# Subtractions and weighted sums on VectorE: one operation over 1024 columns in place of two over 512

## The chip, the cores and the metric

The kernel runs on one core of a Trainium2 chip. The time is device microseconds (us) of one execution; for the kernel before it is 1416.0 us, the median of 3 runs (1414.63 to 1416.56). A change is measured against runs of the kernel before on the same chip.

## The reference

Two layers of one mixer each, on 256 latent tokens and 256 context tokens of 2048 features, all float32:

```python
shift, scale, gate = jnp.split(sc @ w_ada[l] + b_ada[l], 3, axis=-1)       # the same for c_ctx
h_lat = rms_norm(x, norm_g[l]) * (1.0 + scale[:, None]) + shift[:, None]
h_ctx = rms_norm(xc, norm_g[l]) * (1.0 + scale_c) + shift_c
p = h @ w_in                                   # q, k, v, g_gqa, cq, ckv, kr, g_mla
...
o_a = block_attention(q, concat(ctx k, lat k), concat(ctx v, lat v))         # GQA, 8 heads
o_b = block_attention(q_mla, ...)                                            # MLA, 8 heads
x = x + gate[:, None] * (concat(o_a * silu(g_a), o_b * silu(g_b)) @ w_out)
```

In layer 0 the context tokens pass through the same mixer, in layer 1 only their keys and values are needed. A final `rms_norm` ends it. The vectors `shift`, `scale` and `gate` (the modulation) depend on two vectors alone, `c` and `c_ctx`, multiplied by a matrix of 2048 x 6144 per layer.

## The kernel before

**Matmuls in three parts.** Each float32 operand is split into a high part, rounded to the matmul's float32r, and a low part, the rest. `mm3` (L138) issues three matmuls for one product: high by high (L141), and the two mixed ones (L142, L143). A weight tile is made by `wtile` (L105): one DMA of 512 KB into a `raw` buffer (4 buffers), `hi` by a copy on ScalarE (L114, 3 buffers), and `lo = raw - hi` (L116, 2 buffers). The tile has k * w columns per partition, mostly 2 x 512 = 1024, in 48 tiles 2 x 288 = 576, and 512 in the first tiles. `lo` is computed in two halves, two instructions of the same line, each over half the columns. Every fifth tile's `lo` is computed on GpSimd (POOL), the others on VectorE (DVE).

**The modulation in the background.** The first part of layer 0's modulation runs on TensorE at the start (`ada_pe`, L229). Everything else of it, layer 0's gate and all of layer 1's modulation, is a matrix by vector product on DVE (`ada_half`, L252): a row block of the transposed matrix is loaded into a `rad` buffer (128 x 1024, 512 KB, 2 buffers), and for each vector v (two of them, one for layer 1's gate) the products with `cb[:, v]` are summed along the row. This is line L273, one instruction with an accumulator, in NG = 2 halves of 512 columns: the first writes its sum to `o`, the second takes `o` as its start value. Each instruction is followed by a short one that reads the accumulator out. 128 `rad` blocks make 224 sums, so 448 instructions and 448 reads. The products themselves go to a `junk` tile that nobody reads.

**What sets the order.** `ada_rest` is a generator. `wtile` advances it by `bg_rate` steps per weight tile (1.3 in most of layer 0, 0.4 in layer 1), which fixes the place of the sums in the order in which the program is written. A scheduler then orders all instructions by a simulation of its own (`schedule_with_timeline_sim`): on each engine, and on the one DMA queue (SP), an instruction is put where the simulation finds it ready. At run time each engine and the queue take their instructions strictly in that order. A `rad` or `raw` load waits on SP for the last reader of the buffer that it fills, and what is behind it on SP waits too.

**Other names.** `pt` (L147, L148) is the transposed softmax split in two, `p` (L600, L603) the softmax, whose scaling by 1/sum runs on POOL, `sm` (L597, L598, L601) its maxima and sums on DVE, `go` (L810) the gated output projection, `rb` and `ra` (L469, L471) rotary products, `y_d` a store of the finished GQA output, `gate_d` the gates in DRAM. The layer 0 stages in order: input projections by slices of the features (0 to about 230 us), GQA heads beside the remaining projections (230 to 480), MLA projections and heads, and the output projection (to about 835), then layer 1.

Of the kernel before, what the change touches and what calls it, by code (L numbers as in the profile page):

```python
# [35 lines left out]
NB_ACC, NB_ATT = 4, 4  # L36
FILL = (1, 0, 1, 0, 1, 1, 1, 0)
POOL_LO = 5
NG = 2

BGS, BG0, BG1, BG3, BG2 = 5.0, 1.3, 1.1, 0.5, 0.4
TCKW = {"schedule_with_timeline_sim": True}
# [2 lines left out]
def fr(ap):  # L45
    return ap.bitcast(F32)


class Net:
# [55 lines left out]
    def wtile(self, src, k, w):  # L105
        nc = self.nc
        self.nw += 1
        t = self.raw(src, k, w, "rad" if self.start and self.nw % 3 == 0 else "raw")[0][:, : k * w]
        h = self.wp.tile([P, 1024], F32R, tag="hi", name=self.nm("hi"))[:, : k * w]
        lo = self.wp.tile([P, 1024], F32R, tag="lo", name=self.nm("lo"), bufs=NB_LO)[:, : k * w]  # L110
        self.nlo += 1
        e = nc.gpsimd if POOL_LO and self.nlo % POOL_LO == 0 else nc.vector
        n = k * w
        nc.scalar.copy(h, t)  # L114
        for c in (slice(0, n // 2), slice(n // 2, n)):
            e.tensor_tensor(out=lo[:, c], in0=t[:, c], in1=fr(h[:, c]), op=ALU.subtract)  # L116
        self.bg_due += self.bg_rate
        while self.bg and self.bg_due >= 1.0:
            self.bg_due -= 1.0
            self.bg_step()  # L120
        if not self.bg:
            self.bg_due = 0.0
        v = lambda z: z.rearrange("p (k n) -> p k n", k=k)
        return v(h), v(lo)
# [127 lines left out]
    def ada_half(self, half, work):  # L252
# [8 lines left out]
        for l, kind, vs in work:  # L261
# [4 lines left out]
            for k in range(KT):  # L266
                r = self.raw(self.a["w_adaT"][r0 + k * P : r0 + (k + 1) * P, hs], 1, 1024, "rad")[1][:, 0, :]
                for v in vs:
                    o = out[:, k, v : v + 1]
                    for i in range(NG):  # L270
                        cs = slice(i * 1024 // NG, (i + 1) * 1024 // NG)
                        junk = self.tp.tile([P, 1024 // NG], BF16, tag="junk", name=self.nm("junk"), bufs=1)
                        nc.vector.tensor_tensor_reduce(  # L273
# [924 lines left out]
```

## Time and profile before

| | |
|---|---|
| median of 3 runs | 1416.0 us |
| profiled execution, whole | 1413.77 us |
| its span, first to last instruction | 1412.0 us |
| mean granted TensorE clock | 0.984 |
| PE busy | 1331.6 us, 94% |
| DVE busy | 1094.0 us, 77% |
| ACT busy | 602.6 us, 43% |
| POOL busy | 404.0 us, 29% |
| DMA | 272.47 MB, mean 193 GB/s |

Busy times are unions of the instructions' spans on one engine. Matmuls overlap, so a busy PE is not always one at its full pace; the idle time of PE and a granted clock under 1 are what it certainly lost. [...]

### The profile page before, as it was taken

What the parts mean: (1) busy time and instruction counts of PE and PEld (TensorE: products, weight loads), DVE (VectorE), ACT (ScalarE), POOL (GpSimd) and SP (SyncE); (2) the same over time, 40 slices, a digit from 0 to 9 for tenths busy, and PEclk for the clock granted to TensorE, in tenths of its full rate; (3) what the DMA queues carried; (4) which work ended last, traced back from release to release, by engine and by line L of the source; (5) the groups of instructions that cost most, each with busy time, mean ns of one, the idle gap of its engine ahead of it and who ended that gap; (6) DMA issues with size and microseconds to landing.
All of it is one profiled execution on the core that took longest, in us unless ns stands there. A gap on an engine that the chain in (4) does not pass through costs nothing.

```text
span 1412.0 us, 21026 instructions
## 1 busy us (share of the span) xinstructions
PE 1331.6 (94%) x7516; PEld 1128.1 (80%) x7516; DVE 1094.0 (77%) x2297; ACT 602.6 (43%) x974; POOL 404.0 (29%) x385
## 2 busy tenths in 40 slices
PE   5999999999997999898998999999999999999996
PEld 4776787877786987787886778898898989888884
DVE  2776548998887998989998965976787776857566
ACT  4322224535443242455532134665555644454443
POOL 0110015423223130221222213533234431223335
PEclk9999999999999999999999999999999999999999
DMA  9987733455554766443576665655775757733444
GB/s 310 354 276 268 271 104 104 135 164 181 160 187 155 209 217 199 148 147 120 179 247 210 209 214 178 202 161 169 237 257 162 237 156 259 257 108 124 157 139 144
DMA packets 142120, 272.47 MB, mean 193 GB/s; under 512 B 8336, under 2 KB 53824, under 8 KB 140608
## 3 DMA queue, kind: packets, MB, share of 16 engines
q1 hardware_dynamic: 142016, 271.13, 59.5%
q8 instruction: 59, 0.97, 0.3%
q14 instruction: 45, 0.37, 0.1%
HBM read 264.78 MB, written 6.32 MB: 192 GB/s over the span
## 4 chain that ended last, share of the span: by engine, by line
PE 55%; DVE 21%; DMA 11%; issue 6%; ACT 3%; POOL 2%; SPq 1%; DVEq 0%; POOLq 0%; ACTq 0%
PE acc L143 16%; PE acc L141 16%; PE acc L142 15%; DVE junk L273 8%; DMA rad<-in_w_adaT 7%; DVE lo L116 5%; PE att L592 3%; PE att L229 2%; PE att L615 1%; DMA raw<-in_w_in 1%; DMA cb<-in_cr 1%; DVE sm L597 1%; DVE pt L148 1%; DMA ra<-in_w_ada 1%; ACT hi L114 1%
## 5 line engine op out<-in xcount | busy, mean ns | idle before, releaser
L114 ACT CAST hi<-raw 128x1024 fp32r<-128x1024 f32 (+2 forms) x279 | 271.9, 977 | 380.1 <-PE acc L142 206.4
L116 DVE TENSOR_TENSOR lo<-raw,hi 128x512 fp32r<-128x512 f32 (+2 forms) x446 | 307.5, 731 | 88.8 <-PE acc L143 39.5
L116 POOL TENSOR_TENSOR lo<-raw,hi 128x512 fp32r<-128x512 f32 (+2 forms) x112 | 153.4, 1390 | 466.1 <-PE acc L143 317.4
L141 PE MATMUL acc<-hi,h 128*128 128x512 f32 (+1 forms) x672 | 239.3, 359 | 7.4 <-ACT cq L455 4.8
L142 PE MATMUL acc<-hi,h 128*128 128x512 f32 (+1 forms) x672 | 237.7, 356 | 0.0
L273 DVE CUSTOM_DVE_ANT_0 junk<-rad,cb 128x512 bf16<-128x512 f32 x224 | 175.0, 781 | 76.0 <-DMA rad<-in_w_adaT 50.4
L143 PE MATMUL acc<-lo,h 128*128 128x512 f32 (+1 forms) x672 | 227.4, 359 | 2.7 <-DVE lo L116 2.4
L273 DVE CUSTOM_DVE_ANT_0 junk<-rad,cb,as 128x512 bf16<-128x512 f32 x224 | 193.1, 862 | 3.8
L142 PE MATMUL acc<-h,lo 128*128 128x512 f32 (+1 forms) x512 | 171.4, 340 | 2.5 <-DVE lo L116 2.5
L143 PE MATMUL acc<-h,hi 128*128 128x512 f32 (+1 forms) x512 | 170.0, 338 | 0.0
L603 POOL TENSOR_SCALAR p<-p,sm 128x512 f32<-128x512 f32 (+1 forms) x96 | 85.8, 900 | 283.9 <-DVE sm L601 247.9
L141 PE MATMUL acc<-h,hi 128*128 128x512 f32 (+1 forms) x512 | 165.0, 341 | 0.3 <-ACT q L455 0.3
L143 PE MATMUL acc<-lo,y 128*128 128x512 f32 x384 | 146.3, 400 | 9.2 <-DVE lo L116 8.1
L141 PE MATMUL acc<-hi,y 128*128 128x512 f32 x384 | 150.7, 398 | 2.4 <-ACT y L147 2.0
L142 PE MATMUL acc<-hi,y 128*128 128x512 f32 x384 | 151.9, 396 | 0.2 <-DVE y L148 0.2
L141 PEld LDWEIGHTS acc<-hi,h 128*128 128x128 f32 x672 | 127.2, 189 | 28.9 <-ACT cq L455 5.0
L143 PEld LDWEIGHTS acc<-lo,h 128*128 128x128 f32 x672 | 124.6, 189 | 22.3 <-DVE lo L116 4.1
L142 PEld LDWEIGHTS acc<-hi,h 128*128 128x128 f32 x672 | 127.0, 189 | 15.5
L142 PEld LDWEIGHTS acc<-h,lo 128*128 128x128 f32 x512 | 96.8, 190 | 12.8 <-DVE lo L116 3.6
L143 PEld LDWEIGHTS acc<-h,hi 128*128 128x128 f32 x512 | 96.7, 190 | 9.8
L141 PEld LDWEIGHTS acc<-h,hi 128*128 128x128 f32 x512 | 93.6, 190 | 13.0 <-issue 2.5
L143 PEld LDWEIGHTS acc<-lo,y 128*128 128x128 f32 x384 | 73.4, 192 | 28.0 <-DVE lo L116 12.2
(219 smaller groups left out, 2281.4 us busy)
## 6 DMA issues: line engine op xcount, KB each, us to landing
rad<-in_w_adaT SPq DMA_DIRECT2D x128, 512.0 KB, 4.5
raw<-in_w_in SPq DMA_DIRECT2D x125, 512.0 KB, 4.5
raw<-in_w_out SPq DMA_DIRECT2D x72, 512.0 KB, 4.0
ra<-in_w_ada SPq DMA_DIRECT2D x32, 1024.0 KB, 8.4
raw<-in_w_in SPq DMA_DIRECT2D x48, 288.0 KB, 3.1
raw<-in_w_ukv SPq DMA_DIRECT2D x16, 512.0 KB, 3.5
cb<-in_cr SPq DMA_DIRECT2D x6, 1024.0 KB, 7.2
raw<-in_w_uq SPq DMA_DIRECT2D x12, 512.0 KB, 3.7
```

The costliest lines, as they stand in the source:

```text
L114: nc.scalar.copy(h, t)
L116: e.tensor_tensor(out=lo[:, c], in0=t[:, c], in1=fr(h[:, c]), op=ALU.subtract)
L141: mm(out, lhsT=ah, rhs=bh, start=first, stop=False)
L142: mm(out, lhsT=al, rhs=bh, start=False, stop=False)
L143: return mm(out, lhsT=ah, rhs=bl, start=False, stop=last)
L148: self.nc.vector.tensor_tensor(out=lo, in0=src, in1=fr(hi), op=ALU.subtract)
L229: nc.tensor.matmul(ps[32 * g : 32 * g + 32, :], lhsT=self.scp[:, m + i, o : o + 32], rhs=rs[kind, m][:, i, :], start=run is runs[0] and j ...
L273: nc.vector.tensor_tensor_reduce(out=junk, in0=r[:, cs], in1=cb[:, v, cs], scale=1.0, scalar=o if i else 0.0, op0=ALU.mult, op1=ALU.add, a ...
L592: self.order = nc.tensor.matmul(banks[j], lhsT=q[:, qs], rhs=k[:, ks], start=i == 0, stop=i == len(score) - 1)
L597: nc.vector.tensor_reduce(out=nb[:, c], in_=v, axis=AX.X, op=ALU.max)
L603: nc.gpsimd.tensor_scalar(out=pr[j], in0=pr[j], scalar1=l[:, j : j + 1], scalar2=1.0, op0=ALU.mult, op1=ALU.mult)
L615: nc.tensor.transpose(b[:, k, j * P : (j + 1) * P], pr[j][:, (i + k) * P : (i + k + 1) * P], self.ident)
```

## The change

Three edits. On DVE `lo` is computed by one instruction over all k * w columns; on POOL it stays in two halves. NG is 1, so that a sum takes one instruction over 1024 columns and one accumulator read, the start value is always 0.0, and `junk` is 1024 columns wide (2 KB per partition, before 1 KB). The scratch memory for DMA descriptors is set to 2 KB per partition; no DMA of this kernel is issued by POOL.

```diff
-NG = 2
+NG = 1
...
         e = nc.gpsimd if POOL_LO and self.nlo % POOL_LO == 0 else nc.vector
         n = k * w
         nc.scalar.copy(h, t)
-        for c in (slice(0, n // 2), slice(n // 2, n)):
+        for c in (slice(0, n // 2), slice(n // 2, n)) if e is nc.gpsimd else (slice(0, n),):
             e.tensor_tensor(out=lo[:, c], in0=t[:, c], in1=fr(h[:, c]), op=ALU.subtract)
...
-    nc = bacc.Bacc("TRN2", target_bir_lowering=False, num_devices=1)
+    nc = bacc.Bacc("TRN2", target_bir_lowering=False, num_devices=1, dynamic_dma_scratch_size=2048)
```

Since the scheduler simulates the program, the order changes on every engine. The first place is the DMA queue SP in the middle of the GQA heads of layer 0, around the store of the first GQA group (`y_d_94`); `cb` are the vectors of the next group of sums. Before:

```order
L827 DMA lg_3680<-in_lat_gain 128x512
L96 DMA raw_3542<-in_w_in 128x2x512
L96 DMA rad_2702<-in_w_adaT 128x1024
L942 DMA y_d_94<-g_63_382 128x2048
L96 DMA rad_2743<-in_w_adaT 128x1024
L96 DMA rad_2784<-in_w_adaT 128x1024
L96 DMA raw_3583<-in_w_in 128x2x512
L96 DMA rad_2828<-in_w_adaT 128x1024
L96 DMA raw_3624<-in_w_in 128x2x512
L259 DMA cb_2825<-in_cr 128x2x1024
```

And the same place on SP now:

```order
L96 DMA raw_3358<-in_w_in 128x2x512
L96 DMA rad_2691<-in_w_adaT 128x1024
L96 DMA rad_2730<-in_w_adaT 128x1024
L96 DMA raw_3394<-in_w_in 128x2x512
L827 DMA lg_3514<-in_lat_gain 128x512
L259 DMA cb_2727<-in_cr 128x2x1024
L96 DMA rad_2736<-in_w_adaT 128x1024
L942 DMA y_d_94<-g_63_379 128x2048
L96 DMA rad_2772<-in_w_adaT 128x1024
L96 DMA rad_2808<-in_w_adaT 128x1024
L96 DMA raw_3431<-in_w_in 128x2x512
```

The second `cb` load stood behind the store and now stands in front of it: the background has moved ahead of the projections. Counted over the whole queue, 14 `rad` loads from the matrix stood ahead of this store and now 18, 29 and now 38 ahead of the second group's store, and 74 and now 90 ahead of the reload of `y_d` shortly before the output projection, at 41, 51 (now 53) and 94 `raw` loads.

The second place is DVE in the output projection of layer 0, from the last `go` of its first 512 columns to the next `lo`. Before:

```order
L810 TENSOR_TENSOR go_7303<-acc_6822,gt_6790 128x512
L273 ISA junk_6394,as_4354<-rad_6392,cb_5007 128x512
L273 ISA as_4354 128x1
L273 ISA junk_6396,as_4354<-rad_6392,cb_5007,as_4354 128x512
L273 ISA as_4354 128x1
L273 ISA junk_6398,as_4354<-rad_6392,cb_5007 128x512
L273 ISA as_4354 128x1
L273 ISA junk_6400,as_4354<-rad_6392,cb_5007,as_4354 128x512
L273 ISA as_4354 128x1
L273 ISA junk_6404,as_4354<-rad_6402,cb_5007 128x512
L273 ISA as_4354 128x1
L116 TENSOR_TENSOR lo_7392<-raw_7389,hi_7391 128x512 x2
```

And the same place on DVE now, from the second `go` on:

```order
L810 TENSOR_TENSOR go_6827<-acc_6376,gt_6361 128x512
L810 TENSOR_TENSOR go_6838<-acc_6383,gt_6359 128x512
L810 TENSOR_TENSOR go_6850<-acc_6390,gt_6359 128x512
L273 ISA junk_7035,as_4109<-rad_7033,cb_4688 128x1024
L273 ISA as_4109 128x1
L273 ISA junk_7037,as_4109<-rad_7033,cb_4688 128x1024
L273 ISA as_4109 128x1
L116 TENSOR_TENSOR lo_6933<-raw_6930,hi_6932 128x1024
```

Five halves from two `rad` blocks stood between the last `go` and `lo`; now it is two whole sums from one block. Between the four `go`s of this step stood six halves of sums and one pair for `lo`; now there is one `lo` and no sum.

## Rows read from the trace of the kernel before

**Rows 1.** The page, part 1: busy us (share of span) and instructions.
```profile
PE 1331.6 (94%) x7516; PEld 1128.1 (80%) x7516; DVE 1094.0 (77%) x2297; ACT 602.6 (43%) x974; POOL 404.0 (29%) x385
```

**Rows 2.** Windows: stretch; us; PE, PEld, DVE, ACT, POOL busy (x); PE clock; DMA share; GB/s.
```profile
230.00:480.00 250.00, 232.46 (x1228) 198.18 (x1227) 222.23 (x528) 107.55 (x172) 83.34 (x80) 0.97 0.53 167
480.00:835.00 355.00, 332.98 (x1753) 281.81 (x1752) 318.99 (x752) 135.60 (x236) 81.10 (x77) 0.98 0.59 190
835.00:1230.00 395.00, 385.39 (x2371) 344.62 (x2370) 294.63 (x544) 203.63 (x309) 142.56 (x133) 1.00 0.65 208
```

**Rows 3.** Waits of PE, 480 to 835: total us, times, longest us.
```profile
PE acc L143 <- DVE lo L116: 6.9, 4, 3.2
PE acc L141 <- DVE rb L471: 4.7, 2, 2.5
PE att L592 <- ACT p L600: 2.9, 1, 2.9
```

**Rows 4.** Waits in 230 to 480, of PE and of DVE.
```profile
PE att L615 <- POOL p L603: 5.4, 6, 1.8
...
DVE junk L273 <- ACT cb L260: 13.2, 2, 7.9
```

**Rows 5.** The page, part 5: groups xcount | busy us, mean ns | idle before, releaser.
```profile
L116 DVE TENSOR_TENSOR lo<-raw,hi 128x512 fp32r<-128x512 f32 (+2 forms) x446 | 307.5, 731 | 88.8 <-PE acc L143 39.5
...
L273 DVE CUSTOM_DVE_ANT_0 junk<-rad,cb 128x512 bf16<-128x512 f32 x224 | 175.0, 781 | 76.0 <-DMA rad<-in_w_adaT 50.4
```

**Rows 6.** Timeline of DVE, 565 to 573: start us, us, instruction.
```profile
565.29 1.29 DVE L116 TENSOR_TENSOR lo<-raw,hi 128x512 fp32r<-128x512 f32 x2
...
567.17 0.69 DVE L469 TENSOR_TENSOR ra<-acc,k 128x512 f32<-128x512 f32 x1
567.77 0.75 DVE L471 TENSOR_TENSOR rb<-acc,k 128x256 f32<-128x256 f32 x2
568.43 0.68 DVE L273 CUSTOM_DVE_ANT_0 junk<-rad,cb 128x512 bf16<-128x512 f32 x1
...
569.04 3.47 DVE L116 TENSOR_TENSOR lo<-raw,hi 128x512 fp32r<-128x512 f32 x2
```

**Rows 7.** Timeline of POOL, 565 to 573.
```profile
568.59 3.36 POOL L663 TENSOR_TENSOR tw<-ra,rb 128x512 f32<-128x512 f32 x2 [19.04 <-DVE rb L471]
```

**Rows 8.** Timeline of DVE, 766 to 774.
```profile
766.06 0.69 DVE L273 CUSTOM_DVE_ANT_0 junk<-rad,cb 128x512 bf16<-128x512 f32 x1
...
766.80 0.75 DVE L273 CUSTOM_DVE_ANT_0 junk<-rad,cb,as 128x512 bf16<-128x512 f32 x1
767.47 0.08 DVE L273 DVE_READ_ACCUMULATOR2_ANT as<- 128x1 f32 x1
...
769.21 2.34 DVE L116 TENSOR_TENSOR lo<-raw,hi 128x512 fp32r<-128x512 f32 x2
```

**Rows 9.** Windows for line L273 alone: DVE busy us (x, accumulator reads included).
```profile
230.00:480.00 250.00, 128.60 (x311) 0.97 0.53 167
480.00:835.00 355.00, 184.36 (x463) 0.98 0.59 190
```

**Rows 10.** Timeline of PE, 770 to 775.
```profile
771.00 0.50 PE L143 MATMUL acc<-lo,y 128*128 128x512 f32 x1 [3.23 <-DVE lo L116]
...
773.24 0.63 PE L141 MATMUL acc<-hi,y 128*128 128x512 f32 x1
773.67 0.63 PE L142 MATMUL acc<-hi,y 128*128 128x512 f32 x1
```

**Rows 11.** Waits of PE, 835 to 1412.
```profile
PE acc L143 <- DVE lo L116: 2.6, 4, 0.9
PE acc L142 <- DVE lo L116: 2.5, 4, 0.9
```

**Rows 12.** All waits for a rad load, and rad's times from issue to landing.
```profile
DVE junk L273 <- DMA rad<-in_w_adaT: 50.4, 39, 4.2
...
DMA to landing us min/median/max: 3.4/4.6/11.4
```

## The prediction, made before the result was known

> **What bounds the kernel now.** I read the page's first part, then the windows by stage, then the waits of PE in each stage, and last the instructions around the longest waits. The first part shows two engines close to full: PE is busy for 1331.6 of 1412.0 us, DVE for 1094.0 [rows 1]. A shorter DVE instruction is worth something only where PE waits for DVE, so the windows decide. From 835 to 1230 us PE is idle for 395 - 385.4 = 9.6 us at full clock, with DVE at three quarters: nothing to gain there. From 230 to 480 DVE is busy for 222.2 of 250 us, from 480 to 835 for 319.0 of 355, and PE loses there 17.5 and 22.0 us idle, besides the clock: a mean grant of 0.97 and 0.98 costs up to 0.03 x 250 = 7.5 and 0.02 x 355 = 7.1 us [rows 2]. So about 54 us lie on the table in these 605 us, and only the part that DVE causes can go.
>
> What DVE causes is seen in the waits. From 480 to 835 PE waits 6.9 us for `lo`, 4.7 for `rb`, and 2.9 for a softmax that had waited for its inputs [rows 3]; from 230 to 480 the largest wait is 5.4 us for `p`, scaled on POOL as soon as DVE has its sum [rows 4]. One such wait is worth more than its length: at 771.00 PE resumes after 3.23 us without work, and shortly after it issues a matmul every 0.43 us (773.24 to 773.67), with a duration of 0.63 in place of 0.50 or less [rows 10]. That is the lower of the clock's two levels, given after the gap and kept for a while.
>
> **The change part by part.** First the price of one operation. A 512 column operation holds DVE for 567.77 - 567.17 = 0.60 us, two of 256 columns for 568.43 - 567.77 = 0.66 us, so 0.33 each [rows 6]. The 256 further columns cost 0.27 us and the start of an instruction 0.06. An operation of 1024 columns then takes 0.60 + 0.54 = 1.14 us, two halves 1.20. There are 446 / 2 = 223 pairs of `lo` on DVE [rows 5], so this part saves 223 x 0.06 = 13 us of DVE's time over the whole kernel.
>
> [...]
>
> The sums gain more per pair. Two adjacent halves take 766.80 - 766.06 = 0.74 us for the first, since the second waits for its start value, and 767.47 - 766.80 = 0.67 for the second, together 1.41 [rows 8]. A half with another operation behind it takes 569.04 - 568.43 = 0.61 [rows 6]; halves that stand apart cost 0.61 + 0.67 = 1.28. No operation of 1024 columns with an accumulator is in this trace; from the rows it takes 0.61 + 0.54 = 1.15. The saving is 0.13 to 0.26 per sum, with bounds of 0 (if the accumulating operation were slower over long rows) and 0.8 (the mean of 0.781 for one half [rows 5] vanishing whole). I take 0.19, the middle, because both patterns are frequent: 224 x 0.19 = 43 us. Together DVE is freed of about 56 us of 1094.
>
> What happens beside POOL is not saved. With POOL idle a pair of `lo` takes 1.29 us, beside POOL's `tw` 3.47 [rows 6, 7]. Each half seems to wait once for one POOL instruction, 2.18 / 2 = 1.1 us. As long as DVE has work, each POOL instruction will meet one DVE instruction, long or short, so I count the same total of such waits and no gain; POOL will wait 0.54 us longer per meeting.
>
> Now where the time falls. By the order on SP the sums move ahead: 38 blocks instead of 29 are queued ahead of the second group's store, 90 instead of 74 ahead of the output projection. So in the GQA heads, up to that store, 9 more blocks, or 18 more sums, of 1.15 us are to be done, +21 us. The 311 / 4 = 78 sums already there [rows 9] save 78 x 0.13 to 0.26 = 10 to 20. On balance DVE gets 1 to 11 us more work in the stretch where it is already at 222 of 250. Some of it fits into DVE's own idle time (13.2 us of waiting for `cb` alone [rows 4]). I charge 5 us to PE here.
>
> From 480 to 835 both effects add: 116 sums before [rows 9], about 18 of them gone and the rest shorter by 0.19, so DVE loses 18 x 1.34 + 98 x 0.19 = 43 us of 319. Then most of PE's waits for DVE go. In the output projection five halves stood between the last `go` and the `lo` for which PE waited at 767.8; now two whole sums do, 2.3 us in place of 0.61 x 5 = 3.1 plus the wait for one more block, and the four `go`s have none between them, where six halves stood. I let the 6.9 us of `lo` go, half of `rb`'s 4.7 (its rest is POOL's), none of the 2.9, which hangs on a load of `cb`, 2 us of the small ones behind DVE, and 5 of the 7.1 us of clock that these gaps caused: 6.9 + 2.4 + 2 + 5 = 16 us.
>
> Against it stands the first half of `lo`. At 769.21 the pair of `lo` starts and lasts to 771.55, PE resumes at 771.00, so it waits for the first half alone [rows 8, 10]. With one operation its columns are free 0.54 us later. Where PE waits for `lo` with nothing to spare, 8 times after 835 [rows 11], that adds up to 8 x 0.54 = 4.3 us; I take 2, and 1 back for the shorter sums in front. The start and the end of the kernel have no sums and few waits for DVE: 0. Sum: -16 + 5 + 1 = -10 us, from the profiled 1413.8 to 1403.8. The median of the runs shown is 2.2 us above that execution, so 1406 us.
>
> **The rivals.** A: the freed time turns into waiting for `rad`. DVE waits 50.4 us in 39 places for such loads, and one takes 4.6 us to land [rows 12]. With two buffers a block can come every (4.6 + two sums) / 2: (4.6 + 2.7) / 2 = 3.65 us before, (4.6 + 2.3) / 2 = 3.45 after. Where this loop sets the pace, only 0.2 of the 0.4 us saved per block remains; and as DVE is in order, each wait holds back the `lo` and `pt` behind it. The blocks come thicker than before, which speaks for it; from 230 to 835 DVE was held by its own work more than by loads, which speaks against. Half of the 16 us gone, with the 6 us of charges unchanged: 1413 to 1418.
>
> B: slower, through the GQA heads. Here the change puts up to 11 us more work on DVE, the blocks come one every 3 to 4 us, and softmax, `pt` and `lo` stand behind whole sums. If DVE is the bound there and loads add 9 blocks x 1.1 us of waiting, PE loses 11 + 10 = 21 us, less some 9 us that it had lost already; with gaps of 3 us the lower clock adds 3, which makes +15. With 11 of the 16 us from 480 to 835 kept and the 1 us of the late halves, the sum is +5, and with 6 kept it is +10: 1421 to 1426. It decides from the point where PE's idle time from 230 to the last store grows by more than the gain behind it. For it speaks DVE's 89% there, against it that PE's waits in this stretch are on several engines.
>
> C: POOL pays. POOL's scaling of `p` and every fifth `lo` would be late by 0.54 us per meeting. With the 6 waits for `p` [rows 4] and as many elsewhere it costs 12 x 0.54 = 6.5 us, leaving -3.5: 1412.5 us. [...]
>
> **How the numbers follow.** A change under 0.2% (2.8 us) is not told from none, so faster means under 1413.2 and slower over 1418.8. The forecast, with 1398 to 1411, has 0.5; C 0.08, most of it faster; a larger gain, all 29 us of idle and clock from 480 to 835, down to 1387, 0.05; A 0.17, with nearly all of it no change; B 0.2. That gives faster 0.60, same 0.19, slower 0.21. The range for 8 in 10 reaches from 1391 to 1422: it leaves out the far end of the large gain and of B.
>
> **What would show it.** In the profile after, L116 on DVE at about 1.2 us (with POOL active 2.2) and L273 at about 1.2; DVE busy near 1040; from 480 to 835 PE's waits for `lo` under 2 us and a granted clock of 0.99 or more; the stretch up to the second store as long as before or 5 us longer. I am wrong if PE's idle time grows in the GQA heads by more than 10 us, if DVE's waits for `rad` rise over 80 us, or if L273's mean is over 1.6 us, which means that length cost more than the columns.

## The result: slower by 0.7%

The changed kernel takes 1427.59 us (median of 4 runs, 1425.72 to 1428.33), the kernel before beside it 1415.32 (1413.98 to 1416.56). The ratio is 1.007, 95% interval 1.0046 to 1.0094, so 12 us lost where 10 were forecast as gained, and outside the range. The profiled execution has a span of 1426.2 us.

The page's first part after the change, against [rows 1]:

```profile
PE 1333.6 (94%) x7516; PEld 1130.8 (79%) x7516; DVE 991.1 (69%) x1618; ACT 602.5 (42%) x974; POOL 434.7 (30%) x385
```

DVE has 1094.0 - 991.1 = 102.9 us less to do, almost twice the 56 us of the forecast, and POOL 30.7 more. PE does the same work, and the kernel is longer. The windows by stage, against [rows 2]:

```profile
230.00:480.00 250.00, 227.75 (x1147) 190.45 (x1146) 218.23 (x375) 103.55 (x167) 98.76 (x83) 0.95 0.56 177
480.00:835.00 355.00, 330.80 (x1799) 285.28 (x1799) 269.34 (x459) 135.56 (x238) 85.42 (x76) 0.98 0.56 180
```

In the first row PE got through 1147 matmuls in place of 1228, and the granted clock fell from 0.97 to 0.95. In the traces of both kernels the grant at any moment is 1.00 or 0.50, and a value between them is a mean of the two: before, behind the gap of [rows 10], it is 1.00 up to 772 us, 0.50 from 773 to 775, and 1.00 again from 776. Windows by the clock on the wall compare different work once the kernels have drifted apart, so I cut the kernel at two instructions that both have: the second store to `y_d` (end of the GQA heads) and the first matmul of L386 (layer 1's norm). The rows are those of one source line each, with its first and last start; of L942 I take the last, of L386 the first. Before:

```profile
L942 SPq DMA_DIRECT2D y_d<-g x2: 330/376/423, 326.3 to 413.5; - x2
...
L386 PE MATMUL att<-k,xn x64: 270/272/275, 888.0 to 926.2; 128*128 128x128 f32 x64
```

After:

```profile
L942 SPq DMA_DIRECT2D y_d<-g x2: 330/334/338, 336.1 to 441.3; - x2
...
L386 PE MATMUL att<-k,xn x64: 270/273/328, 901.2 to 937.6; 128*128 128x128 f32 x64
```

Up to the second store the kernel lost 441.3 - 413.5 = 27.8 us. From there to layer 1's norm it gained: 901.2 - 441.3 = 459.9 in place of 474.5, so 14.6. From there to the end 525.0 in place of 524.0.

The two cuts don't hold quite the same work, as the windows of PE show (matmuls in the first bracket). Before:

```profile
0.00:413.50 413.50, 385.04 (x2150) 304.91 (x2151) 311.46 (x672) 159.60 (x258) 99.53 (x106) 0.98 0.64 208
413.50:888.00 474.50, 444.93 (x2319) 378.41 (x2319) 402.96 (x924) 175.77 (x295) 117.79 (x108) 0.97 0.59 190
```

After, and two matmuls from a stretch at the full clock (445 to 455 us, granted clock 1.00):

```profile
0.00:441.30 441.30, 402.34 (x2183) 317.32 (x2184) 320.39 (x562) 162.61 (x260) 108.99 (x106) 0.96 0.65 211
441.30:901.20 459.90, 431.56 (x2286) 370.07 (x2285) 331.33 (x534) 170.60 (x290) 126.06 (x107) 0.98 0.56 181
```

```profile
449.02 0.39 PE L142 MATMUL acc<-hi,h 128*128 128x512 f32 x1
449.25 0.39 PE L143 MATMUL acc<-lo,h 128*128 128x512 f32 x1
```

In the changed kernel 33 matmuls of the projections have moved in front of the second store. At one every 0.23 us that is, as an estimate, 7.6 us of work, so on equal work some 20 us are lost in front of the store and some 7 gained behind it. In front of it PE's idle time grew from 28.5 to 39.0 us, and the clock's fall from 0.98 to 0.96 costs up to 0.04 x 441.3 - 0.02 x 413.5 = 9.4 us more, an estimate as well.

What stood there, by PE's waits from 230 to 480, against [rows 4]:

```profile
PE att L615 <- POOL p L603: 6.9, 6, 2.3
PE att L143 <- DVE pt L148: 5.0, 3, 3.0
PE att L592 <- DVE qT L148: 4.9, 1, 4.9
```

Of these the wait for `qT` is new. The one for `pt` was smaller before:

```profile
PE att L143 <- DVE pt L148: 2.2, 2, 1.1
```

One timeline of DVE shows how the wait for `pt` comes about (start us, us, instruction):

```profile
314.83 2.07 DVE L273 CUSTOM_DVE_ANT_0 junk<-rad,cb 128x1024 bf16<-128x1024 f32 x1
...
316.97 2.17 DVE L273 CUSTOM_DVE_ANT_0 junk<-rad,cb 128x1024 bf16<-128x1024 f32 x1
...
319.18 1.60 DVE L273 CUSTOM_DVE_ANT_0 junk<-rad,cb 128x1024 bf16<-128x1024 f32 x1
...
320.92 1.49 DVE L273 CUSTOM_DVE_ANT_0 junk<-rad,cb 128x1024 bf16<-128x1024 f32 x1
...
322.35 0.41 DVE L623 TENSOR_TENSOR g<-att,g 128x256 f32<-128x256 f32 x1
...
323.28 1.21 DVE L273 CUSTOM_DVE_ANT_0 junk<-rad,cb 128x1024 bf16<-128x1024 f32 x1
...
324.50 1.21 DVE L116 TENSOR_TENSOR lo<-raw,hi 128x1024 fp32r<-128x1024 f32 x1
325.63 0.68 DVE L148 TENSOR_TENSOR pt<-att,pt 128x512 fp32r<-128x512 f32 x1
326.23 1.21 DVE L273 CUSTOM_DVE_ANT_0 junk<-rad,cb 128x1024 bf16<-128x1024 f32 x1
327.37 0.08 DVE L273 DVE_READ_ACCUMULATOR2_ANT as<- 128x1 f32 x1
```

Four sums stand in front of the gating `g`, a fifth and a `lo` in front of `pt`, with no idle time between. PE waits for both, 0.41 us for `g` and 2.98 for `pt`; the last row is its later wait for `qT`:

```profile
322.90 0.36 PE L141 MATMUL att<-pt,v 128*128 128x256 f32 x1 [0.41 <-DVE g L623]
...
326.36 0.39 PE L143 MATMUL att<-pt,v 128*128 128x256 f32 x1 [2.98 <-DVE pt L148]
...
342.98 1.65 PE L592 MATMUL att<-kT,qT 128*128 128x512 f32 x3 [4.90 <-DVE qT L148]
```

The wait for `qT` goes back to the `cb` load that has moved in front of the store, as the order on SP had shown. DVE and ScalarE, one after the other:

```profile
335.66 0.42 DVE L623 TENSOR_TENSOR g<-att,g 128x256 f32<-128x256 f32 x1 [0.40 <-PE att L143]
341.09 1.23 DVE L273 CUSTOM_DVE_ANT_0 junk<-rad,cb 128x1024 bf16<-128x1024 f32 x1 [5.00 <-ACT cb L260]
...
342.24 1.28 DVE L148 TENSOR_TENSOR qT<-att,qT 128x512 fp32r<-128x512 f32 x2
```

```profile
337.85 1.28 ACT L260 ACT_TABLE_LOAD   x1 [3.31 <-DMA cb<-in_cr]
339.14 1.91 ACT L260 ACTIVATE cb<-cb 128x2048 f32<-128x2048 f32 x1
340.96 1.54 ACT L147 CAST qT<-att 128x512 fp32r<-128x512 f32 x3
```

ScalarE stands for the load, the casts of `qT` behind it; DVE stands at a sum that needs `cb`, with the `qT` for which PE waits queued behind that sum.

### The profile page after: what moved, and what is told of

The parts are those of the page before. It is cut to its first block, busy times and chain, and to the rows that moved or that the text cites. A ratio compares the mean times of both kernels' runs of the same rounds, so it can differ in the third digit from the quotient of the medians.

```text
span 1426.2 us, 20239 instructions
## 1 busy us (share of the span) xinstructions
PE 1333.6 (94%) x7516; PEld 1130.8 (79%) x7516; DVE 991.1 (69%) x1618; ACT 602.5 (42%) x974; POOL 434.7 (30%) x385
## 4 chain that ended last, share of the span: by engine, by line
PE 56%; DVE 17%; DMA 10%; issue 6%; POOL 5%; ACT 3%; SPq 1%; DVEq 0%; POOLq 0%; ACTq 0%
PE acc L141 16%; PE acc L142 16%; PE acc L143 16%; DVE junk L273 7%; DMA rad<-in_w_adaT 5%; DVE lo L116 3%; PE att L592 3%; DMA cb<-in_cr 2%; PE att L229 2%; POOL lo L116 1%; PE att L615 1%; DMA raw<-in_w_in 1%; DVE sm L597 1%; DVE pt L148 1%; DMA ra<-in_w_ada 1%
## 5 line engine op out<-in xcount | busy, mean ns | idle before, releaser
L273 DVE CUSTOM_DVE_ANT_0 junk<-rad,cb 128x1024 bf16<-128x1024 f32 x224 | 297.3, 1327 | 99.0 <-DMA rad<-in_w_adaT 71.2
L116 DVE TENSOR_TENSOR lo<-raw,hi 128x1024 fp32r<-128x1024 f32 (+2 forms) x223 | 266.2, 1196 | 138.6 <-PE acc L143 69.5
L116 POOL TENSOR_TENSOR lo<-raw,hi 128x512 fp32r<-128x512 f32 (+2 forms) x112 | 147.3, 1336 | 419.3 <-PE acc L143 256.1
L143 PE MATMUL acc<-lo,h 128*128 128x512 f32 (+1 forms) x672 | 224.1, 359 | 5.3 <-DVE lo L116 4.1
L603 POOL TENSOR_SCALAR p<-p,sm 128x512 f32<-128x512 f32 (+1 forms) x96 | 102.6, 1075 | 293.3 <-DVE sm L601 239.7
L141 PEld LDWEIGHTS acc<-hi,y 128*128 128x128 f32 x384 | 72.1, 188 | 19.4 <-ACT y L147 2.8
```

Of the source, the lines that this page charges most:

```text
L141: mm(out, lhsT=ah, rhs=bh, start=first, stop=False)
L143: return mm(out, lhsT=ah, rhs=bl, start=False, stop=last)
L273: nc.vector.tensor_tensor_reduce(out=junk, in0=r[:, cs], in1=cb[:, v, cs], scale=1.0, scalar=o if i else 0.0, op0=ALU.mult, op1=ALU.add, a ...
L603: nc.gpsimd.tensor_scalar(out=pr[j], in0=pr[j], scalar1=l[:, j : j + 1], scalar2=1.0, op0=ALU.mult, op1=ALU.mult)
```

## The experiments

Ratios are against runs of the kernel before on the same chip. "Order" is the sequence of the instructions on each engine, as the scheduler drew it or as the kernel fixes it.

| | operations | order | us | ratio, 95% |
|---|---|---|---|---|
| after | whole | drawn | 1427.6 | 1.007 (1.0046 to 1.0094) |
| e1 | `lo` whole | drawn | 1421.1 | 1.0031 (1.0019 to 1.0043) |
| e2 | sums whole | drawn | 1423.0 | 1.0039 (1.0014 to 1.0063) |
| e3 | whole | drawn, other rates | 1436.9 | 1.0158 (1.0129 to 1.0188) |
| e4 | halves | drawn (as before) | 1415.9 | 0.9994 (0.9973 to 1.0016) |
| e5 | whole, 2 loads of `cb` | drawn | 1425.7 | 1.0085 (1.0057 to 1.0112) |
| e6 | halves, 2 loads of `cb` | drawn | 1398.4 | 0.9882 (0.9851 to 0.9913) |
| e7 | as e5 | drawn, e3's rates | 1436.2 | 1.0151 (1.0114 to 1.0189) |
| e8 | halves | drawn, rates nudged | 1419.9 | 1.0017 (0.9994 to 1.004) |
| **e9** | **whole** | **of before** | **1392.6** | **0.9837 (0.9806 to 0.9868)** |
| **e10** | **halves** | **of after** | **1482.8** | **1.047 (1.0439 to 1.0501)** |
| e11 | as e5 | of e6 | 1378.2 | 0.9734 (0.9708 to 0.976) |
| e12 | whole | sums at before's places | 1398.3 | 0.9871 (0.984 to 0.9902) |
| e13 | whole | PE's of before | 1424.8 | 1.0065 (1.0039 to 1.0091) |
| e14 | whole | DVE's of before | 1410.6 | 0.9957 (0.9939 to 0.9976) |
| e15 | whole | drawn for quarters | 1444.9 | 1.0193 (1.0158 to 1.0229) |
| e16 | whole | as e12, 8 sums ahead | 1414.5 | 0.999 (0.9972 to 1.0009) |
| e17 | whole | as e12, 18 sums ahead | 1415.3 | 0.9992 (0.9974 to 1.0011) |
| e18 | as e5 | sums at e6's places | 1387.1 | 0.9804 (0.9787 to 0.9822) |

**e1 to e4: one part of the change, or its pace.** e1 has the second edit of the diff alone, e2 NG = 1 and the scratch, e4 the scratch alone. e3 is the whole change with

```diff
-BGS, BG0, BG1, BG3, BG2 = 5.0, 1.3, 1.1, 0.5, 0.4
+BGS, BG0, BG1, BG3, BG2 = 5.0, 0.85, 1.35, 1.4, 0.4
```

> Only the subtraction is done in one operation; the sums stay in two halves, and in the order they stand where they stood before (64 pairs ahead of the 60th weight tile, as before; 82 with the whole change). Theory PACE (the loss comes from the sums having moved ahead of the projections in layer 0): no loss, 1410 to 1417 us, DVE busy about 1075. Rival LENGTH (a whole operation of 1.2 us holds up what stands behind it, and POOL, wherever it stands): about half of the loss, 1418 to 1423 us.

> Only the sums are done in one operation; the subtraction stays in halves. In the order the sums move ahead as with the whole change (82 pairs ahead of the 60th tile). PACE: all of the loss, 1424 to 1431 us, with PE's idle time and half clock growing from 230 to 690 us. LENGTH: half of it, 1419 to 1424.

> The whole change, but the rates at which the sums are emitted are 0.85, 1.35 and 1.4 per weight tile in place of 1.3, 1.1 and 0.5, so that they stand in the order about where they stood before the change (58 pairs ahead of the 60th tile, 116 ahead of the 90th; before 64 and 119). PACE: the loss is gone and the freed DVE time shows, 1402 to 1413 us. LENGTH: still 1424 or more. Third theory CB (the loads of the vectors cb happened to fall where PE waits for what stands behind them on ACT and DVE, 11.3 us against 7.7): 1418 to 1427, by where they fall now.

> Before with the descriptor scratch of 2 KB alone, the same instructions in the same order. All theories: 1413 to 1418 us, no difference.

The scratch costs nothing (e4, ratio 0.9994). The two halves of the change add up, 0.31% + 0.39% against 0.7%, each about half as LENGTH had said, and slowing the sums down made it worse. I believed LENGTH then. It was wrong, and these runs could not have shown it: every edit of a length also makes the scheduler draw another order. e3's rates change more than the sums' places: they also issue each `rad` load later, and from the first GQA head to the second store DVE then stood for loads in 12 places:

```profile
DVE junk L273 <- DMA rad<-in_w_adaT: 17.9, 12, 3.9
```

In that stretch of the changed kernel it is 3.1 us in 4 places.

**e5 to e8: `cb`, and the draw.** e5 and e7 (and, with halves, e6) keep the two `cb` tiles:

```diff
-        return self.tp.tile([P, 2, 1024], F32, tag="cb", name=self.nm("cb"), bufs=1)
+        return self.tp.tile([P, 2, 1024], F32, tag="cb", name=self.nm("cb"), bufs=2)
...
-        cb = self.cb_tile()
-        with self.behind():
-            nc.sync.dma_start(out=cb, ...)
-        nc.scalar.activation(cb, cb, AF.Silu)
+        if half not in self.cbs:
+            self.cbs[half] = self.cb_tile()
+            with self.behind():
+                nc.sync.dma_start(out=self.cbs[half], ...)
+            nc.scalar.activation(self.cbs[half], self.cbs[half], AF.Silu)
+        cb = self.cbs[half]
```

> The whole change, but the broadcast rows cb of the two halves (loaded and put through Silu three times each, in one buffer) are kept in two buffers, so 2 loads instead of 6; the sums then run still further ahead (90 pairs ahead of the 60th weight tile, against 82 after the change and 64 before). CB (what was lost are the places where ScalarE and VectorE stand in order behind a load of cb): both stalls of 5 to 6 us at 338 and 569 us are gone, total 1413 to 1419. LENGTH (the 1.2-us operation holds up whatever is queued behind it): about as after, 1422 to 1428, with the stage of the GQA heads still 15 us or more over before. ORDER (sums taken ahead of the projections' work, whatever their length): 1428 or more, since they are taken further ahead still.

> The same two buffers of cb, scratch of 2 KB, but sums and low parts in halves of 512 as before; the order puts 89 pairs ahead of the 60th weight tile, as far as e5 does. So e5 and e6 differ in the length of the operations and hardly in how far the sums are ahead. LENGTH: as before or faster, 1406 to 1416, and 8 us or more under e5. ORDER: slower than before like the whole change, 1424 to 1432, and VectorE's larger load makes it no faster than e5. CB: below before, 1405 to 1412.

> e5 with the sums spread by the rates 0.85, 1.35, 1.4 (58 pairs ahead of the 60th weight tile; e3's rates). CB: the stage of the GQA heads at before's length and no stall behind cb, 1410 to 1420. ORDER: 1410 to 1420 as well, as the sums are not ahead, and then 8 us or more under e5. LENGTH: 1422 or more, as e3 and e5.

> The kernel before with its rates 1.3, 1.1, 0.5 set to 1.25, 1.05, 0.55: every operation has before's length and there are as many; the order is the same up to the end of the GQA heads and differs behind them. REDRAW (the order that the scheduler draws is worth several us either way, and before's constants were fitted to its own draw): 3 us or more from before, more likely slower, 1418 to 1424. LENGTH, ORDER and CB: no change, 1414 to 1418.

CB gets no support as the whole cause: without four of the six loads e5 is no faster, though its order is drawn anew too. It may be worth something where the order is good: e6 is 1.2% under before, but its order is another too. e5 and e6 are 27 us apart with about as many sums ahead, which looked like the proof of LENGTH: again both orders were drawn. e8 can't be told from no change.

**e9 to e11: the order held.** A table gives each engine's order, and every instruction is queued behind the one ahead of it in the table:

```diff
         build(tc, a)
+        pin(tc, nc)
...
+        for x in struct.unpack("<%dh" % (len(d) // 2), d):
+            r += x
+            if prev is not None:
+                tc.add_manual_dep(ins[r], prev.name, mybir.DependencyInfo(mybir.DependencyClass.NoSync, mybir.DependencyReason.DATA))
+            prev = ins[r]
```

> The whole change, but the instructions of every engine (and the DMA issues) are queued one behind the other in the order of the kernel before, a whole operation in the place of the first of its two halves. So e9 differs from before in the length of the operations alone. LENGTH: most of the loss stays, 1421 to 1430. ORDER (what was lost is the order that the scheduler drew for the changed lengths): no loss, and the forecast's gain comes, 1400 to 1412.

> The counterpart: halves of 512 as before (scratch of 2 KB), but all engines queued in the order of the changed kernel, the two halves side by side in the place of the whole operation. It differs from before in the order alone. ORDER: the loss is there, 1424 to 1434. LENGTH: no loss, 1408 to 1418; under before if the order with the sums ahead is the better one, as e6 (1398) suggests.

> e5 (whole operations, two buffers of cb) with every engine queued in e6's order: it differs from e6 (1398) in the length of the operations alone. LENGTH: 1415 to 1426, most of the 27 us between e6 and e5. ORDER: 1390 to 1402, as e6 or under it, since VectorE has some 90 us less to do.

This settles it between LENGTH and ORDER. In before's order the whole operations are 1.6% faster, some 23 us, better than the forecast. In the changed kernel's order the halves are 4.7% slower, some 67 us. So whole operations are the faster in either order, by 1.6% in before's and by 1.047 - 1.007 = 4.0% in the changed kernel's, and before's order is the faster with either length. It costs the changed kernel 1.007 - 0.9837 = 2.3%, 33 us, to have its own. e9's windows, against those of after:

```profile
230.00:480.00 250.00, 238.75 (x1295) 205.49 (x1294) 209.95 (x356) 109.14 (x175) 99.55 (x81) 0.99 0.56 175
480.00:835.00 355.00, 338.47 (x1778) 287.49 (x1777) 290.84 (x481) 139.20 (x240) 96.52 (x77) 0.99 0.59 193
```

148 more matmuls than after in the first row, at a clock of 0.99, with fewer operations of DVE. e11 is the version that beats both kernels, by 2.7% against before.

**e12 to e15: which part of the order.** In e12 only the sums are held, each behind the operation of DVE that it followed in the kernel before; e13 and e14 hold one engine; e15 holds all, in an order drawn for four operations of 256 columns.

> The changed kernel with one set of edges more: each sum on VectorE is queued behind the operation that it followed in the kernel before; all else is drawn freely (TensorE's order stays nearly as far from before's as the changed kernel's is). AHEAD (the sums taken ahead are the loss): 1390 to 1402, as e9. TIGHT (TensorE's order, drawn for results that VectorE should have early, is the loss): 1420 to 1438, as after and e3.

> The changed kernel with TensorE alone queued in the order of before; the other engines are drawn freely, and the sums run ahead as in the changed kernel (80 pairs ahead of the 60th weight tile, 64 before, 82 after). TIGHT: 1390 to 1405. AHEAD: 1420 to 1430.

> The changed kernel with VectorE alone queued in the order of before, TensorE drawn freely. AHEAD: 1390 to 1402. TIGHT: over e13 by 8 us or more, 1410 to 1430. If e12, e13 and e14 all stay over 1410, it is the fit of the engines' orders to each other and not one engine's.

> The changed kernel with all engines queued in the order that is drawn for operations of 256 columns (four for each tile; 49 pairs of sums ahead of the 60th weight tile, and the last sums reach into the output projection). TIGHT (an order drawn for more time on VectorE than it then takes gives slack): no worse than e9, 1380 to 1396. AHEAD: sums now lie behind before's places, so 1385 to 1400 up to the output projection, and there some us back. If the order of before is good for a reason of its own (its constants), 1405 or more.

The sums' places take 1.007 - 0.9871 = 2.0% away, 28 of the 33 us, with what the scheduler then draws around them: the other engines' order and that of the loads change too. TensorE's order of before takes nothing from the total. It moves the loss: e13's second store starts at 419.9 us, with 2135 matmuls ahead of it in place of 2183, and layer 1's norm at 897.4, so the stretch between takes 477.5 us in place of 459.9. From the first head of layer 0 to 345 us, before and after:

```profile
244.00:345.00 101.00, 95.56 (x490) 80.21 (x489) 95.04 (x231) 49.25 (x83) 37.68 (x36) 0.97 0.50 157
```

```profile
244.00:345.00 101.00, 86.60 (x423) 71.63 (x422) 86.64 (x153) 43.92 (x73) 39.89 (x35) 0.91 0.55 175
```

and e12:

```profile
244.00:345.00 101.00, 98.08 (x512) 82.19 (x511) 88.97 (x162) 50.76 (x86) 42.94 (x39) 1.00 0.53 167
```

DVE is as busy in e12 as after the change, and PE gets through 512 matmuls in place of 423, at a clock of 1.00. Its waits in this stretch of e12:

```profile
PE att L615 <- POOL p L603: 1.4, 2, 1.1
PE att L522 <- DVE qT L148: 0.8, 1, 0.8
```

In the changed kernel the same stretch has 5.0 us for `pt`, 4.9 for `qT` and 3.4 for `p`. DVE waits for `cb` in e12 as well, up to 5.8 us at a time from 244 us to the second store, against 5.6 after the change: what counts is what stands behind. With no other edit than the sums' places the cut gives the lengths that the forecast had wanted:

```profile
L942 SPq DMA_DIRECT2D y_d<-g x2: 330/360/390, 324.2 to 413.6; - x2
...
L386 PE MATMUL att<-k,xn x64: 270/273/329, 873.6 to 910.0; 128*128 128x128 f32 x64
```

413.6 us to the second store, as before and with as much work (2153 matmuls against 2150), and 460.0 from there to layer 1's norm in place of 474.5. e14 came out 8 us above AHEAD's range: DVE's whole order, with a TensorE order drawn around it, is worse than the sums' places alone. The fit between engines counts too, but TensorE's order by itself (e13) is not the loss. e15 shows that late is no better than early. Layer 1's norm needs the sums, and from 835 to 960 PE has

```profile
PE att L386 <- ACT f L377: 47.4, 1, 47.4
```

behind ScalarE's

```profile
928.72 1.02 ACT L377 ACTIVATE f<-att,mod,mod 128x256 f32<-128x256 f32 x2 [39.01 <-DVE f L375]
```

where DVE had its last sum for it at 926.41. So TIGHT, as a rule that an order drawn for longer operations is the safer one, falls for the whole kernel. Up to layer 1's norm it isn't excluded: e15 reaches the first matmul of L386 at 867.7 us, e9 at 867.6, and all that e15 loses against e9 lies from there on.

**e16 to e18: how far, or where.** As e12, with each sum's place taken from the sum 8 or 18 before it; e18 is e12's edit on e5.

> As e12 (each sum queued behind an operation of VectorE, all else free), but each sum is held behind the operation that the 8th sum before it had followed in the kernel before. 68 sums then lie ahead of the 60th weight tile and 127 ahead of the 90th (e12 64 and 119, after 82 and 147). COUNT (the loss grows with how far the sums run ahead): 1403 to 1412. PLACES (the loss comes from sums packed between the urgent operations, not from their number): 1394 to 1403.

> The same by 18 sums: 81 ahead of the 60th weight tile, as after the change, but 136 ahead of the 90th (after 147) and 158 ahead of the 97th (after 178). COUNT: 1415 to 1426. PLACES: 1398 to 1410.

> e5 (whole operations, two buffers of cb, 1426) with only the sums held behind the operations that they followed in e6. AHEAD, as e12 showed it: 1380 to 1395, near e11 (1378). If e12 was a lucky draw: 1410 or more.

e18 repeats e12's finding on another base: 1425.7 to 1387.1 us. It also speaks against the count: 78 sums stand ahead of its second store and 80 ahead of e5's, and it gets there at 421.5 us, e5 at 441.1. e16 and e17 fit neither theory whole: both lie over PLACES' ranges, and 8 sums ahead cost as much as 18, which COUNT excludes, though e17 by itself lies in COUNT's range. In both the first group of heads is that of the changed kernel again (423 and 421 matmuls from 244 to 345, clock 0.91 and 0.90). e17's second store starts at 440.9 us, as after the change, and yet e17 is 12 us faster: it needs 446.5 us from there to layer 1's norm, where the changed kernel needs 459.9. So the sums' places matter behind the store too. I read the loss as a cost of single collisions, such as the stack in front of `pt` and the `cb` load in front of the store, which 8 sums are enough to bring. No run takes these two apart by an edit. The `cb` load isn't needed for a loss of this size: e5 issues its last one at 270.6 us, reaches the second store as late as the changed kernel, and PE waits there once for 4.10 us for `g`, which stands behind sums and a `lo`. Why the scheduler prefers such places was not tried.

## Why the prediction was wrong

**The step that failed: "I charge 5 us to PE here."** For the GQA heads the forecast counted DVE's work: 18 sums more, each shorter, 1 to 11 us on balance, partly in idle time. Measured, the second store comes 27.8 us later, and some 20 us of that are lost on equal work. It is no matter of load: from 244 to 345 us DVE is busy for 86.6 us in the changed kernel and 89.0 in e12, and PE differs by 89 matmuls. What counts is what stands in front of the operation that PE waits for, and for that DVE need only be in order. The rows on SP had shown it before the run, a `cb` load that moved from behind the first store to in front of it. The text used them to count blocks and did not ask what stands behind this load on ScalarE and DVE: `qT`, and a wait of 4.9 us.

**The gain behind it: the size came near by luck, its mechanism did not come.** From the second store to layer 1's norm the forecast was -16 and the cut shows -14.6, but some 7.6 us of that are the projections that had moved ahead. 11.3 us of PE's waits were to go there; its idle time between the cuts went from 29.6 to 28.3 us. The waits from 480 to 835, against [rows 3]:

```profile
PE acc L141 <- DVE g L457: 6.4, 1, 6.4
...
PE acc L142 <- DVE lo L116: 2.0, 1, 2.0
...
PE acc L143 <- DVE lo L116: 1.6, 1, 1.6
```

The step "I let the 6.9 us of `lo` go" failed: 3.6 us stayed, and a new wait came in, of the same kind as in the GQA heads. DVE waits for a `cb` load, five sums follow, and PE waits for the `g` behind them:

```profile
566.22 1.22 DVE L273 CUSTOM_DVE_ANT_0 junk<-rad,cb 128x1024 bf16<-128x1024 f32 x1 [7.04 <-ACT cb L260]
...
575.34 0.77 PE L141 MATMUL acc<-hi,cqT 128*128 128x512 f32 x1 [6.37 <-DVE g L457]
```

In e9, the fast kernel in before's order, PE waits more for `lo` from 480 to 835 than before, so its gain isn't that term either:

```profile
PE acc L143 <- DVE lo L116: 8.0, 4, 3.2
```

Behind layer 1's norm the forecast was +1 and measured +1.0, less than the 2.6 us by which runs of the changed kernel differ. With the GQA heads at before's length (e12) the kernel is 18 us faster than before, 1.29%. In e9 all stages gain, and in place of the 5 us charge the second store comes 6.5 us earlier (407.0), some 3 of them for 14 matmuls that moved behind it.

**The price of an operation held, the saving was too small.** All sums of the changed kernel, min/median/max in ns, and in front of them the first and second halves before:

```profile
L273 DVE CUSTOM_DVE_ANT_0 junk<-rad,cb x224: 669/691/1786, 252.2 to 1232.8; 128x512 bf16<-128x512 f32 x112
L273 DVE CUSTOM_DVE_ANT_0 junk<-rad,cb,as x224: 730/752/1854, 255.2 to 1233.5; 128x512 bf16<-128x512 f32 x112
```

```profile
L273 DVE CUSTOM_DVE_ANT_0 junk<-rad,cb x224: 1197/1224/2320, 255.2 to 1244.7; 128x1024 bf16<-128x1024 f32 x112
```

The distance from one start to the next is 325.63 - 324.50 = 1.13 us for `lo` and 327.37 - 326.23 = 1.14 for a sum, against 1.14 and 1.15 worked out. But DVE's busy time fell by 102.9 us, not 56. The groups, against [rows 5]:

```profile
L273 DVE CUSTOM_DVE_ANT_0 junk<-rad,cb 128x1024 bf16<-128x1024 f32 x224 | 297.3, 1327 | 99.0 <-DMA rad<-in_w_adaT 71.2
L116 DVE TENSOR_TENSOR lo<-raw,hi 128x1024 fp32r<-128x1024 f32 (+2 forms) x223 | 266.2, 1196 | 138.6 <-PE acc L143 69.5
```

A pair of `lo` beside POOL took 3.47 us [rows 6]; the longest whole sums, at 261.45 and 1048.53 us, take 2.32, their own 1.2 and 1.1 more, beside POOL's `q` (L516, L478). So "the same total of such waits" was wrong. Time above the median of their own kind, of which the wait beside POOL is the part seen here, was (781 - 691) + (862 - 752) = 200 ns per pair of halves of a sum, 45 us in all (862 is the mean of the second halves), and is 1327 - 1224 = 103 ns per whole sum, 23 us; for `lo` it went from 41 to 15 us. These 48 us and the 56 of the forecast make 104, close to the 102.9 measured: half as many operations run over by less in all.

**The rivals.** B had the right place and sign at 0.2, with +15 us for the stage where 27.8 came, some 20 of them on equal work; its reason, more load on DVE, was not the one. A: waits for `rad` rose from 50.4 to 71.2 us, under the 80 set as the bound, and e9 is fast with 55.9. C: POOL does pay, 434.7 us busy in place of 404.0, but in e9 it is 446.5, in the faster kernel, so this isn't the loss. No run shows C's 0.54 us per meeting by itself: POOL's scaling of `p` (L603) went from a mean of 900 to 1075 ns, its halves of `lo` (L116) from 1390 to 1336.

**What would have shown it.** Of the signs named, L116 and L273 at about 1.2 us came, and DVE's busy time went below the 1040, to 991.1. From 480 to 835 PE's waits for `lo` were 3.6 us, not under 2, and the clock stayed at 0.98. Of the signs for being wrong none came by the letter: PE's idle time from 230 us to the second store grew from 10.0 to 18.1 us, short of the 10 us named, and the clock's fall in that stretch, from 0.98 to 0.94, was no part of the sign.

## What to carry to other kernels

Where a scheduler draws the order, a change of an operation's length is two changes. Hold the old order and time the new lengths, then the other way round, before saying which of them paid; comparisons of two drawn kernels agreed here with the wrong theory three times over (e1 with e2, e3, e5 with e6). In a forecast, look in the new order for what now stands in front of each operation that the bounding engine waits for, above all an operation that itself waits for a load, and price it by the whole wait; the engine's total load says little about it.

## What the runs showed of the hardware

The same instructions, only queued differently, took 1392.6 us (before's order), 1427.6 (as drawn) and 1444.9 (drawn for quarters) with whole operations, and 1415.3 (as drawn) and 1482.8 (after's order) with halves. The longest whole sum took 1.1 us over the median of 1.22, as the longest half of a pair (1.79) did over 0.69. All 12 whole sums over 2.1 us, and before all halves of sums over 1.6, ran beside an instruction of POOL: there a whole sum runs over by about as much as a half, and half as many of them by less in total, 23 us in place of 45. Where PE's waits were longer the clock was lower too: from 244 to 345 us the mean grant is 0.91 in the changed kernel, with the waits of 3.0 and 4.9 us, and 1.00 in e12, where no wait exceeded 1.1.
